# Column quarters for the sums of the front, and the last round, the norm, the gates and the heads' loads in another order

## The chip, the cores and the metric

The kernel runs on one core of a Trainium2 chip. Time is the device time of one execution in microseconds (us); the median over several runs is compared. The core has five engines that each take their instructions in order: PE (matmuls, with weight loads as PEld), VectorE (DVE), ScalarE (ACT), GpSimd (POOL) and SyncE (SP). SP, ACT and POOL also issue DMAs; SP and ACT have hardware queues, POOL a software queue.

## The reference

A trunk of two layers over a sequence of 1024 tokens of width 1024, in float32. Every sub-layer takes `h = rms(x) * g * (1 + scale) + shift`, where scale, shift and gate come from the conditioning vector c by a matrix-vector product (`silu(c) @ w + b`).

```python
# layer 0: S5 mixer
u, z = split(h @ w_in)                      # 1024 -> 2 x 1024
s = scan(abar, bbar @ u); y = C @ s + D * u # 64 groups of 16 channels, 64 complex states
y = gelu(y); y = y * sigmoid(y @ w_glu + b_glu) * silu(z)
x = x + gate * (y @ w_out)
# shared: k, v, forget gates from x;  k = head_rms(k);  F = cumsum(log_sigmoid(f + bias))
# layer 1: attention, 16 heads of 64
q, z = split(h @ w_in); q = head_rms(q) / 8
o = softmax(q k' + F_q - F_k, causal) v;  x = x + gate * ((o * silu(z)) @ w_out)
```

## The kernel before

All activations lie transposed: a strip is 128 channels by 1024 tokens, in two halves of 512 tokens. To keep accuracy with the fast matmul type, every weight and activation is split into a high part (ScalarE's copy, `aH`, `w_hi`) and a low part (VectorE's subtraction, `aL`, `w_lo`), and each product is three matmuls, high by high, high by low, low by high (`project_part`, L108). `weight_strip` (L82) loads a strip of weights through SP and splits it.

The order on each engine is made by the framework's planner: it walks the program with a timeline of estimated costs and gives each engine a fixed order. `tc.issue_after(ins)` adds an edge in that order, on the engine of `ins` alone: what is written inside the block comes behind `ins` on that engine. It is no wait on a semaphore.

The stages, in order of time, with the names in the profile:

1. The front (L127 to L377). For each of eight strips of x, SP loads one matrix of scale weights (`mwx`) and the strip (`xt`); VectorE reduces the product of the matrix with silu(c), a copy of c on all partitions (`gemv`, L131), to 128 values of scale; ScalarE and VectorE make `aH` and `aL` scaled by them, without the norm; ScalarE squares the strip (`sqx`) and PE sums the squares over all channels by a matmul with a constant matrix (`msx`, L298), for both halves. The factor of the norm, `q2x`, is -2/rms, multiplied onto the result of the projections (`et`, L333). The shift is handled as two more token columns (`aH`, `aL`, L311 and L312) next to the second half: PE runs a projection in three chunks of 512, 256 and 258 columns, and the last gives the bias `bi`. Strips 0 to 3 of u are projected before the S5 loop (`U_FIRST`), strips 0 and 1 straight from the front in PSUM tiles of their own (`u01`). Beside it VectorE makes the coefficients of the S5 layer, `dt`, `mag` (a power on POOL, L228), angles `th`, their sine and cosine, powers `pwr`, `pwi`, and the matrices `bb`, `bbs`. They start on VectorE as soon as `ldt`, `are`, `aim` are loaded, and those from `th` on are gated behind `last_lo`, the last shift column.
2. The S5 loop (L680 to L703): eight turns; `products`, `tables`, `scan` and `rotate_back` on VectorE (`moa`, `wm`, `sT`, `r`), small matmuls on PE (`pin`, `pk`, `vps`, `py`), swaps of partition halves by DMA (`v`). `unit()` puts the remaining projections between them, a third of a strip at a time. `taps` (L579) holds matmuls that use 32 columns of PE each, at four places.
3. The gated unit (L752 to L775): `pj_g`, `zt` and `yt` loaded back from memory, `sg`, `zs`.
4. The output projection (L786 to L814), 16 tiles in the order `OUT_SEQ`: all of half 0 is done after the twelfth. `x1` is the new residual; its squares are summed on POOL (`acc`), and `ms` gives the mean of a half.
5. Keys, values, queries (L831 to L970): `modulated` makes `aH` and `aL` of all eight strips and both halves; before it VectorE and POOL in turn multiply `x1` by `q2` in place (L834). Six jobs, `v0 v2 k0 k2 q0 q2`, each of two wide weight strips and eight token tiles (`tkps`, L861, 24 matmuls of 128 x 256). Values go to memory (`vt`, `v_d`), keys and queries are squared, averaged and raised to -1/2 on POOL (`hms`), multiplied (`hnt`), transposed (`trps`), split (`kh`, `kl`) and stored. After `v0` `forget_gates` runs. The other 48 matrices of scale and shift are loaded by `mod_load` and reduced by `mod_take` along stages 3 to 5, 16 of them in `v0` and `v2`. In `q0`, `modulated` runs again for the queries.
6. Attention (L1155 to L1174): 64 steps of one head and 256 queries, two steps of `scores` ahead (`LOOK`). `head` (L989) loads a head's keys, queries and values, mostly by POOL. `some_fill` puts parts of the z projection (`zb`) and of the first rows of the last projection (`f`) between the steps: 8 parts at each of three places at the start, then 2 a step.
7. The last projection (`pj_f`, L1184) and the stores.

The lines that the change touches and what calls them:

Of the kernel before, what the change touches and what calls it, by code (L numbers as in the profile page):

```python
# [37 lines left out]
F_ROWS, Z_END = 2, 2  # L38
# [7 lines left out]
def trunk(tc, a, out):  # L46
# [3 lines left out]
    with top:  # L50
# [20 lines left out]
        vecs = ctile([P, 98], "vecs")  # L71
        c_b = modp.tile([P, D], F32, name="c_b", tag="c_b", bufs=1)
        Q.dma_start(out=c_b, in_=a["c"].broadcast_to([P, D]))
        Q.dma_start(out=vecs, in_=a["vecs"])
        vec, at0 = {}, 0
        for nm, w in (("a_g", 8), ("kv_g", 8), ("b_g", 8), ("b_glu", 8), ("kg", 1), ("qg", 1), ("modb", 64)):
            vec[nm] = vecs[:, at0:at0 + w]
            at0 += w
# [3 lines left out]
        def weight_strip(src, shape, l_eng=None, pool=None):  # L82
            raw = (pool or wpool).tile(shape, F32, name="w_raw", tag="w_raw", bufs=2 if pool else 1)
            Q.dma_start(out=raw, in_=src)
# [5 lines left out]
        def copy_on(eng, o, i):  # L90
            if eng is S:
                S.activation(o, i, AF.Copy)  # L92
# [5 lines left out]
        def split(x, hi, lo, h_eng=None, l_eng=None):  # L98
            copy_on(h_eng or S, hi, x)
            (l_eng or V).tensor_tensor(out=lo, in0=x, in1=hi.bitcast(F32), op=ALU.subtract)  # L100
# [7 lines left out]
        def project_part(ps, w, act, half, ks, k0=0, k1=KT - 1):  # L108
            for k in ks:
                for n, (wt, at) in enumerate(((0, 0), (0, 1), (1, 0))):  # L110
                    T.matmul(ps, w[wt][:, k, :], act[at][k][half], start=(k == k0 and n == 0), stop=(k == k1 and n == 2))  # L111

        def project(w, act, half, nm):
            ps = pj.tile([P, HL], F32, name="pj_" + nm, tag="pj")
            project_part(ps, w, act, half, range(KT))
# [20 lines left out]
        def mod_load(behind):  # L136
            n = mod_next[0]
            if n < 64:
                mw = mwp.tile([P, D], F32, name="modw", tag="modw")
                with tc.issue_after(behind):  # L140
                    Q.dma_start(out=mw, in_=a["modw"][n])
# [30 lines left out]
        def modulated(x, k, i, s, sh, act, pool=None, l_eng=None):  # L172
# [19 lines left out]
        with l0:  # L192
# [8 lines left out]
            S.dma_start(out=ldt, in_=a["log_dt"])  # L201
# [1037 lines left out]
```

## Time and profile before

| | us |
|---|---|
| median of 3 runs | 1207.44 (1205.32 to 1210.37) |
| the profiled execution | 1206.17 |
| its span in the profile | 1204.4 |
| PE busy | 1153.0 (96%), 7414 matmuls |
| VectorE busy | 854.5 (71%) |
| ScalarE busy | 606.3 (50%) |
| POOL busy | 376.0 (31%) |
| granted clock of PE, mean | 0.987 |

A row of instructions begins with its start and duration in us, or, in a grouped view, with its line; then come engine, line, operation and `out<-in`; `xN` is the count; in brackets or behind the bar stand the idle time before it and what released it. A row of stretches gives the length, then for each engine its busy time and (x) its instructions, the granted share of PE's clock, the busy share of the DMA engines and GB/s. Matmuls overlap in the pipeline, so a matmul's duration is longer than the distance to the next one.

### The profile page before, as it was taken

The numbers are of one execution on the slowest core, as the hardware profiler recorded it, in microseconds if no ns is written. First come the engines' busy times: TensorE is split into PE (matmuls) and PEld (weight loads), VectorE is DVE, ScalarE is ACT, GpSimd is POOL, SyncE is SP. The second block draws the span as 40 slices with busy tenths as digits, with TensorE's granted clock in tenths as the row PEclk, the third lists the DMA queues.
The fourth block names the chain that finished last, engine by engine and source line by source line (L and its number), as shares of the span: only waits on it lengthen the run. The fifth ranks groups of instructions, "written<-read, shape, count | busy, mean of one in ns | idle before, by whom it ended". The sixth has DMA issues, their size and how long they took to land.

```text
span 1204.4 us, 20401 instructions
## 1 busy us (share of the span) xinstructions
PE 1153.0 (96%) x7414; PEld 1020.9 (85%) x7414; DVE 854.5 (71%) x1725; ACT 606.3 (50%) x1140; POOL 376.0 (31%) x586
## 2 busy tenths in 40 slices
PE   8989998997999998899999999999999999999898
PEld 6879887886788786889999989998888898888686
DVE  7889899885399877875444664347888788887421
ACT  6666766665335234322223443237677777885310
POOL 4000000000000234510044483437576665764100
PEclk9999999998999999999999999999999999999999
DMA  9754556584976894467524275527696978951342
GB/s 359 222 175 128 164 167 163 158 218 151 328 231 192 281 324 140 148 190 248 179 74 173 106 143 165 131 84 151 102 157 112 136 118 112 155 92 27 100 162 79
DMA packets 110388, 197.09 MB, mean 164 GB/s; under 512 B 17136, under 2 KB 58224, under 8 KB 108752
## 3 DMA queue, kind: packets, MB, share of 16 engines
q1 hardware_dynamic: 83072, 153.25, 40.3%
q0 software_dynamic: 25216, 37.76, 19.4%
q10 hardware_dynamic: 2000, 4.79, 1.6%
q8 instruction: 59, 0.97, 0.4%
q14 instruction: 41, 0.34, 0.1%
HBM read 138.21 MB, written 46.27 MB: 153 GB/s over the span
## 4 chain that ended last, share of the span: by engine, by line
PE 67%; DVE 13%; ACT 8%; DMA 4%; issue 4%; POOL 2%; SPq 1%; ACTq 0%; POOLq 0%; DVEq 0%
PE tkps L861 17%; PE u L274 7%; PE pj_o L111 6%; PE pj_f L111 6%; PE zb L111 5%; PE pj_g L111 5%; PE tp L1065 4%; PE ov L1072 3%; PE ov L1071 3%; PE sp L1033 2%; PE sp L1034 2%; PE z L274 2%; DVE r L207 1%; DVE w_lo L100 1%; PE f L111 1%
## 5 line engine op out<-in xcount | busy, mean ns | idle before, releaser
L861 PE MATMUL tkps<-wvh,aH 128*128 128x256 f32 (+1 forms) x768 | 220.6, 288 | 5.5 <-DVE flog L875 4.8
L861 PE MATMUL tkps<-wvl,aH 128*128 128x256 f32 (+1 forms) x768 | 217.3, 284 | 0.0
L861 PE MATMUL tkps<-wvh,aL 128*128 128x256 f32 (+1 forms) x768 | 217.0, 283 | 0.2 <-POOL aL L177 0.2
L861 PEld LDWEIGHTS tkps<-wvh,aH 128*128 128x128 f32 x768 | 145.9, 190 | 6.9 <-issue 5.4
L861 PEld LDWEIGHTS tkps<-wvl,aH 128*128 128x128 f32 x768 | 146.0, 190 | 0.3 <-issue 0.2
L861 PEld LDWEIGHTS tkps<-wvh,aL 128*128 128x128 f32 x768 | 145.5, 190 | 0.7 <-POOL aL L177 0.4
L1067 ACT ACTIVATE pth<-tp 128x512 fp32r<-128x512 f32 (+1 forms) x192 | 87.0, 488 | 56.8 <-PE ov L1071 30.6
L1040 ACT ACTIVATE pr<-pr,mx 128x128 f32<-128x128 f32 (+7 forms) x128 | 98.8, 773 | 22.6 <-DVE mx L1037 21.1
L1042 POOL TENSOR_SCALAR pr<-pr,sm 128x128 f32<-128x128 f32 (+7 forms) x128 | 95.9, 758 | 43.5 <-DVE sm L1041 41.5
L1068 DVE TENSOR_TENSOR ptl<-tp,pth 128x512 fp32r<-128x512 f32 (+1 forms) x192 | 101.2, 552 | 10.6 <-ACT pth L1067 10.1
L92 ACT ACTIVATE w_hi<-w_raw 128x1024 fp32r<-128x1024 f32 x49 | 51.6, 1054 | 90.5 <-PE pj_f L111 29.1
L1037 DVE CUSTOM_DVE_ANT_0 pr<-sp,msk 128x512 f32<-128x512 f32 (+3 forms) x128 | 72.7, 569 | 23.8 <-PE tp L1065 21.0
L1071 PE MATMUL ov<-pth,vhl 128*128 128x256 f32 x320 | 85.8, 300 | 0.2
L1065 PE MATMUL tp<-ident,pr 128*128 128x128 f32 x576 | 84.2, 275 | 1.1 <-DVE ptl L1068 1.0
L885 ACT ACTIVATE hsq<-tkps 128x256 f32<-128x256 f32 x64 | 24.5, 383 | 116.2 <-PE tkps L861 111.0
L1072 PE MATMUL ov<-ptl,vhl 128*128 128x256 f32 x320 | 81.0, 286 | 0.2
L1065 PEld LDWEIGHTS tp<-ident,pr 128*128 128x128 f32 x576 | 69.3, 141 | 11.5 <-DVE ptl L1068 2.7
L1033 PE MATMUL sp<-kk,qs 128*128 128x256 f32 (+2 forms) x192 | 71.5, 375 | 2.8 <-DVE mx L1037 2.4
L888 POOL TENSOR_TENSOR hms<-hms,nhalf 128x4 f32<-128x4 f32 x64 | 68.7, 1074 | 5.0
L890 DVE TENSOR_TENSOR hnt<-tkps,hms 128x256 f32<-128x256 f32 x64 | 27.0, 422 | 60.2 <-POOL hms L888 60.1
L1034 PE MATMUL sp<-kk,q 66*128 66x256 f32 (+2 forms) x192 | 66.2, 348 | 0.0
L887 POOL TENSOR_SCALAR hms<-hms 128x4 f32<-128x4 f32 x64 | 13.0, 203 | 165.2 <-DVE hms L886 164.1
(328 smaller groups left out, 3264.0 us busy)
## 6 DMA issues: line engine op xcount, KB each, us to landing
modw<-modw SPq DMA_DIRECT2D x48, 512.0 KB
wvr<-kvq_w SPq DMA_DIRECT2D x12, 1024.0 KB
mwx<-modw SPq DMA_DIRECT2D x16, 512.0 KB
w_raw<-a_w_in SPq DMA_DIRECT2D x16, 512.0 KB
v_d<-vt SPq DMA_DIRECT2D x32, 256.0 KB
kk<-k_d POOLq DMA_DIRECT2D x16, 512.0 KB, 7.6
vhl<-v_d POOLq DMA_DIRECT2D x16, 512.0 KB, 8.6
qs<-q_d POOLq DMA_DIRECT2D x32, 256.0 KB, 5.1
```

What stands on the lines that cost most here:

```text
L111: T.matmul(ps, w[wt][:, k, :], act[at][k][half], start=(k == k0 and n == 0), stop=(k == k1 and n == 2))
L274: m = T.matmul(ps[:, 0:c1 - c0], w[wt][:, k, :], act[at][k][i][:, c0:c1], start=(k == 0 and n == 0), stop=(k == KT - 1 and n == 2)).ins
L861: T.matmul(ps[:, 0:nv], at, wt[:, k, 0:nv], start=(n == 0), stop=(n == 3 * KT - 1))
L1033: T.matmul(sp[:, 0:wm_], qsl, kk[:, 0, lo:lo + wm_], start=True, stop=False)
L1034: T.matmul(sp[:, 0:wm_], q1_[:, P * i:P * i + P], kk[0:HD + 2, 1, lo:lo + wm_], start=False, stop=True)
L1040: S.activation(pr[:, 0:nk], pr[:, 0:nk], AF.Exp, scale=-1.0, bias=mx, accum_out=sm)
L1042: G.tensor_scalar(out=pr[:, 0:nk], in0=pr[:, 0:nk], scalar1=sm, scalar2=0.0, op0=ALU.mult, op1=ALU.add)
L1065: T.transpose(out=tp[:, b, :], in_=prs[qi][:, P * (b0 + b):P * (b0 + b) + P], identity=ident)
L1067: S.activation(pth[:, 0:m, dst], tp[:, 0:m, :], AF.Copy)
L1068: V.tensor_tensor(out=ptl[:, 0:m, dst], in0=tp[:, 0:m, :], in1=pth[:, 0:m, dst].bitcast(F32), op=ALU.subtract)
L1071: T.matmul(ov, vhl[:, b, :], pth[:, b - b0, :], start=(b == 0), stop=False)
L1072: end = T.matmul(ov, vhl[:, b, :], ptl[:, b - b0, :], start=False, stop=(b == nb - 1)).ins
```

## The change

In order of the stages:

- Front. The sums of squares of four strips are made together: `quarters` issues four matmuls, each with 32 columns of the constant matrix and a strip of its own, whose outputs lie in four groups of 32 partitions of one PSUM tile; two rounds cover eight strips. A copy to SBUF (`mq`) and one matmul with 1/32 (`o32`) for each half bring the groups together. The eight matrices of the shift are stored in another layout (`mod_sh`) and multiplied on PE by silu(c) in the same way (`psh`, two rounds for each half), copied (`shr`) and brought to columns by eight small matmuls (`pm`), in place of eight of VectorE's reductions. The second weight strip has a raw buffer of its own, and both strips are loaded near the start. The loads and the first small instructions of the coefficients come behind `lo_end`, the last `aL` of the front, and the gate of `th` becomes `lo_end` too; these loads go by POOL, `vecs` by ScalarE. Strips 2 and 3 use the PSUM tiles that strips 0 and 1 leave. B and C are loaded behind the weights of strip 3.
- `neg2_rsqrt` reads PSUM directly and has one ScalarE instruction fewer.
- S5 loop: one more `unit` before the last `states_out`.
- Gated unit and output projection take PSUM tiles from `psa` (three buffers) instead of `pj` (two); loads of z and y are chained in order of use; the mean of half 0 is placed in the middle of the next projection.
- `modulated` multiplies by scale and `q2` in one instruction, adds the shift on ScalarE for the high part and in a second fused instruction for the low one; the products in place and POOL's part fall away. Half 0 for the keys and values runs behind the last `w_lo` of the output projection, half 1 behind value tiles 2 to 5 of `v0`.
- Matrices 16 to 39 are reduced in stages 3 and 4, and 40 to 63 in `v2`, `k0` and `k2`. `v0` has none.
- Values are stored by POOL from four buffers; `forget_gates` runs in steps between tiles of `v2`.
- Heads are loaded by SP, all of them. Eight parts of the z projection come before the last normalisation of `q2`.
- The last projection's row 2 is begun among the fill (`F_ROWS` 3), with its weights in a buffer of the keys, and the last four steps take four parts each (`Z_END` 4).

```diff
-F_ROWS, Z_END = 2, 2
+F_ROWS, Z_END = 3, 4
...
+        def project(w, act, half, nm, pool=None, tag="pj", between=None):
+            ps = (pool or pj).tile([P, HL], F32, name="pj_" + nm, tag=tag)
+            m = project_part(ps, w, act, half, range(KT // 2))
+            if between:
+                with tc.issue_after(m):
+                    m = between()
...
         def neg2_rsqrt(v, r, ps, o):
-            S.activation(v, ps, AF.Identity, bias=eps_t)
-            S.activation(r, v, AF.Ln)
+            S.activation(r, ps, AF.Ln, bias=eps_t)
             S.activation(r, r, AF.Exp, scale=-0.5)
-            V.tensor_tensor(out=v, in0=v, in1=r, op=ALU.mult)
+            V.scalar_tensor_tensor(out=v, in0=ps, scalar=EPS, in1=r, op0=ALU.add, op1=ALU.mult)
...
-            S.activation(act[0][k][i], x[k][:, sl], AF.Identity, scale=s[:, k:k + 1], bias=sh[:, k:k + 1])
-            V.tensor_scalar(out=h, in0=x[k][:, sl], scalar1=s[:, k:k + 1], scalar2=sh[:, k:k + 1], op0=ALU.mult, op1=ALU.add)
-            (l_eng or V).tensor_tensor(out=act[1][k][i], in0=h, in1=act[0][k][i].bitcast(F32), op=ALU.subtract)
+            V.scalar_tensor_tensor(out=h, in0=x[k][:, sl], scalar=s[:, k:k + 1], in1=q2[:, sl], op0=ALU.mult, op1=ALU.mult)
+            S.activation(act[0][k][i], h, AF.Identity, bias=sh[:, k:k + 1])
+            V.scalar_tensor_tensor(out=act[1][k][i], in0=h, scalar=sh[:, k:k + 1], in1=act[0][k][i].bitcast(F32),
+                                   op0=ALU.add, op1=ALU.subtract)
...
+            def quarters(ps, ws, xs, first, last):
+                m = T.matmul(ps[96:P, :], ws[3], xs[3], start=first, stop=last).ins
+                with tc.issue_after(m):
+                    for q in range(3):
+                        T.matmul(ps[32 * q:32 * q + 32, :], ws[q], xs[q], start=first, stop=last)
...
-                for i in range(2):
-                    T.matmul(mps[i], onesm, sq[:, HL * i:HL * i + HL], start=(k == 0), stop=(k == KT - 1))
+                if k % 4 == 3:
+                    for i in range(2):
+                        quarters(mps[i], [onesm[:, 0:32]] * 4, [t[:, HL * i:HL * i + HL] for t in sqs[-4:]], k == 3, k == KT - 1)
...
+            for i in range(2):
+                T.matmul(mps[i], o32, mq[:, HL * i:HL * i + HL], start=True, stop=True)
...
-                last_mod = mod_tile(k)
+                    last_mod = Q.dma_start(out=mws[k], in_=a["mod_sh"][k])
...
+                        quarters(psh, [cs[:, k] for k in range(4 * r, 4 * r + 4)],
+                                 [t[:, HL * c:HL * c + HL] for t in mws[4 * r:4 * r + 4]], r == 0, r == 1)
+                S.activation(shr[:, HL * c:HL * c + HL], psh, AF.Copy)
+            for k in range(KT):
+                T.matmul(pm[:, 2 * k:2 * k + 2], shr[:, P * k:P * k + P], o32[:, 0:2], start=True, stop=True)
...
-            gate.enter_context(tc.issue_after(last_lo))
+            gate.enter_context(tc.issue_after(lo_end))
...
-                    unit(1 if more else 2)
+                    unit(1 if more else 3)
...
-                ps = project(held[e][1], act, i, f"o{e}_{i}")
+                ps = project(held[e][1], act, i, f"o{e}_{i}", psa, "psa", pending)
...
-            for i in range(2):
-                sl = slice(HL * i, HL * i + HL)
-                for k in range(KT):
-                    (G if k % 2 else V).tensor_tensor(out=x1[k][:, sl], in0=x1[k][:, sl], in1=q2[:, sl], op=ALU.mult)
-                    modulated(x1, k, i, s_kv, sh_kv, act, xnp, G if k % 3 == 1 else V)
+            for k in range(KT):
+                with tc.issue_after(last_part):
+                    modulated(x1, k, 0, s_kv, sh_kv, act, xnp)
...
-                vt = wv.tile([P, 4, 2, HD], F32R, name="vt", tag="vt")
+                vt = hp.tile([P, 4, 2, HD], F32R, name="vt", tag="kh" if t % 2 else "kl")
...
+                                if job == "v0" and i == 0 and 2 <= n < 6:
+                                    for k in (2 * n - 4, 2 * n - 3):
+                                        with tc.issue_after(end):
+                                            modulated(x1, k, 1, s_kv, sh_kv, act, xnp)
...
-                            if t % 2:
+                            if t % 2 and job != "v0":
                                 mod_take(end, 1)
-                                mod_load(wide_dma[-1])
+                                mod_load(wide_dma[-1], 8 * KT)
...
+                            if job == "q2" and i and d:
+                                for _ in range(Z_FIRST):
+                                    with tc.issue_after(last_nt[-3]):
+                                        behind_z = next(z_fill)
...
-            G.dma_start(out=kk[0:HD], in_=k_d[:, rows, :].rearrange("a d t -> d a t"))
-            G.dma_start(out=kk[HD:P, 0], in_=k_d[0, rows, :])
+            Q.dma_start(out=kk[0:HD].bitcast(F32), in_=k_d[:, rows, :].rearrange("a d t -> d a t"))
+            Q.dma_start(out=kk[HD:P, 0].bitcast(F32), in_=k_d[0, rows, :])
...
+            if e == 2 and e not in wf:
+                w = at0.tile([P, 2, KT, P], F32R, name="wf2", tag="kk")
+                raw = wpool.tile([P, KT, P], F32, name="w_raw", tag="w_raw", bufs=1)
+                Q.dma_start(out=raw, in_=a["b_w_out"][e])
+                wf[e] = w[:, 0], w[:, 1]
+                split(raw, *wf[e])
```

More of the change, by code (lines that the diff above doesn't have):

```diff
@@ L200, in trunk @@
             ldt = tmp.tile([NG, 1], F32, name="ldt")
-            S.dma_start(out=ldt, in_=a["log_dt"])
-            for hh in range(2):
-                S.dma_start(out=are[64 * hh:64 * hh + 64], in_=a["A_re"])
-                S.dma_start(out=aim[64 * hh:64 * hh + 64], in_=a["A_im"])
             def tt(o, x, y, op, eng=V):
@@ L344, in u_strip @@
                     else:
-                        ps, m = (done[c], None) if c < 2 and done else chunk(w, c, f"u{e}")
+                        ps, m = (done[c], None) if c < 2 and done else chunk(w, c, f"u{e}", tags[c])
                         if c == 2:
```

267 lines of the change are left out of this document (166 added, 101 removed).

## The prediction

> **What bounds the kernel now.** I read the page first, then the busy time by stretches, then who waited for whom, then the timeline around each hole.
>
> ```profile
> span 1204.4 us, 20401 instructions
> ...
> PE 1153.0 (96%) x7414; PEld 1020.9 (85%) x7414; DVE 854.5 (71%) x1725; ACT 606.3 (50%) x1140; POOL 376.0 (31%) x586
> ```
>
> PE, at 96%, is the bound. The change removes hardly any matmul, so its worth is the time in which PE stands still, and the time in which it runs at half its clock behind such a hole. These stretches show both; the column after POOL is the granted clock.
>
> ```profile
> 60.00:75.00 15.00, 11.83 (x62) 10.04 (x61) 13.92 (x45) 9.97 (x23) 0.00 (x0) 0.89 0.50 160
> 125.00:140.00 15.00, 13.50 (x88) 11.22 (x87) 12.75 (x16) 9.83 (x16) 0.78 (x1) 0.89 0.55 169
> 265.00:290.00 25.00, 18.13 (x111) 16.63 (x110) 11.16 (x12) 8.57 (x13) 1.06 (x2) 0.86 0.57 186
> 320.00:335.00 15.00, 12.73 (x55) 9.99 (x54) 8.37 (x12) 4.26 (x6) 0.00 (x0) 1.00 0.99 303
> 475.00:500.00 25.00, 19.00 (x105) 15.82 (x104) 23.82 (x29) 9.70 (x15) 16.47 (x13) 0.93 0.43 132
> 500.00:545.00 45.00, 41.34 (x323) 40.13 (x322) 32.40 (x59) 15.01 (x27) 11.37 (x7) 0.96 0.62 197
> 650.00:700.00 50.00, 50.00 (x402) 48.74 (x401) 33.33 (x58) 23.53 (x38) 22.89 (x31) 1.00 0.23 87
> 755.00:770.00 15.00, 12.29 (x92) 12.09 (x92) 6.38 (x10) 3.49 (x6) 9.05 (x14) 0.89 0.77 176
> 800.00:825.00 25.00, 23.71 (x144) 20.68 (x142) 16.57 (x53) 12.41 (x31) 11.00 (x22) 0.86 0.30 107
> 1120.00:1136.00 16.00, 12.37 (x61) 8.57 (x61) 8.54 (x13) 5.02 (x9) 2.46 (x4) 1.00 0.33 114
> ```
>
> Behind the length come the busy times of PE, the weight loads, VectorE, ScalarE and POOL. A hole costs the length less PE's busy time, plus the length times the missing share of the clock: at 60: 3.2 + 1.7 = 4.9 us; 125: 1.5 + 1.7 = 3.2; 265: 6.9 + 3.5 = 10.4; 320: 2.3; 475 to 545: 6.0 + 3.7 idle and 1.8 + 1.8 clock = 13.3; 755: 2.7 + 1.7 = 4.4; 800: 1.3 + 3.5 = 4.8; 1120: 3.6. That is 47 us, and a better order of the same work can gain little more. What ended these holes (total, count and longest, in us):
>
> ```profile
> PE py L639 <- DVE r L207: 8.2, 3, 6.9
> PE pk L579 <- DVE moa L207: 5.0, 6, 1.7
> PE tkps L861 <- DVE flog L875: 4.8, 3, 1.8
> PE pj_o L111 <- DVE w_lo L100: 4.1, 2, 3.0
> PE trps L897 <- DVE hnt L890: 3.2, 3, 2.7
> ```
>
> In all five VectorE was late; work for PE was there.
>
> The Trainium skill, "TensorE: Matmul & The Clock Gate", Part 1, has the half clock follow idle gaps of about its window, some 3.4 us. Here it also followed the stretch at 755, with 2.7 us of idle time in all. By that rule the 1.7 us of clock there would not hang on the hole, and the sum below would be 1.7 us smaller; the trace's row decides.
>
> **The front, to the start of the S5 loop.** The first fence is from the chain of waits, the others from the timeline.
>
> ```profile
> 17.58 1.76 PE msx L298 x4
> ```
>
> ```profile
> 85.11 0.60 PE L567 MATMUL pin<-ident,wm 128*128 128x128 f32 x4
> 85.64 0.43 PE L579 MATMUL pk<-moa,bb 128*32 128x128 f32 x8
> 85.99 0.40 PE L581 MATMUL pk<-dd,ident 128*128 128x16 f32 x2
> ...
> 90.30 1.92 PE L604 MATMUL vps<-uu,min__963 128*128 128x128 f32 x15
> ```
>
> ```profile
> 9.58 10.58 POOL L228 TENSOR_TENSOR mag<-ebase,adt 128x64 f32<-128x64 f32 x1 [3.23 <-DVE adt L207]
> ...
> 35.17 1.41 DVE L293 SCALAR_TENSOR_TENSOR aL<-xt,s_a,aH 128x512 fp32r<-128x512 f32 x2 [1.51 <-ACT aH L292]
> ...
> 50.37 0.21 DVE L207 TENSOR_TENSOR th<-aim,dt 128x64 f32<-128x64 f32 x1
> ```
>
> The mean of squares takes 1.76 us per strip of x today, 14.1 us for eight. The kernel already has matmuls on column quarters: four of them (L579, eight records) start at 85.64 and the next full one (L581) at 85.99, so 0.35 us; eight records of that width on the whole array (L604, 0.128 each) would be 1.02. Quarters run beside each other, at 0.34 of the full price. A group of four at 512 columns costs at least 0.88 us (two records at msx's 0.44) and at most 3.52 (all eight in a row); scaled by 0.34 it is 1.2, which I take. Four groups for the mean (4.8), two closing matmuls (1.8), four groups for the shift (4.8) and 16 small records at L604's price (2.1) are 13.5 against 14.1. PE gains 0.6 us; at the bounds it gains 3.2 or, serial, loses 18.
>
> VectorE loses eight of sixteen reductions; the same one elsewhere (L131, quoted below) takes 1.22 us: 9.8 us off. The small coefficient work moves from before the end of L293 (36.6) to behind it, and the coefficient chain, which today starts at 50.4 (th, behind the last shift columns), can start near 38. Queued behind the new wait are the power on POOL, 10.6 us (mag), now from about 38 to 49, and all that needs it. B and C stand one weight load later in SP's queue, ScalarE gives its first load to vecs, and the coefficients' loads move from ScalarE's queue to POOL's; none of these is needed before 49. But pin (85.1) also needs PE to be through strips 0 to 3. From 36.6 on PE's work was 48.5 us with the hole of 4.9. In the new order PE enters with about 3 us more of strips 0 and 1 done, and has the closing matmuls, the shift and 1.2 us groups ahead of it. So I take 1 us of gain, bounds -3 and 4; if VectorE's 9.8 us covered nothing, 0.
>
> **The S5 loop and its end.** With VectorE some 8 us ahead, part of the waits of pk (5.0) and of the hole at 125 (3.2) goes: 5, bounds 0 and 9. At 265 one more third of a strip stands before the last output, so it covers part of py's 6.9 us: 3 of 10.4, bounds 0 and 7.
>
> **Gated unit and output projection.** Three PSUM buffers instead of two, and z's loads chained ahead of y's: the 2.3 us at 320, bounds 0 and 3.
>
> **From the output projection into the values.** Timeline first, then the chain, then the groups by line:
>
> ```profile
> 469.28 1.06 ACT L92 ACTIVATE w_hi<-w_raw 128x1024 fp32r<-128x1024 f32 x1 [3.19 <-PE pj_o L111]
> ...
> 503.79 0.38 ACT L872 ACTIVATE vt<-tkps 128x256 fp32r<-128x256 f32 x1 [6.42 <-DMA v_d<-vt]
> ```
>
> ```profile
> 479.75 1.15 DVE w_lo L100
> 480.89 0.04 issue
> 480.94 6.78 PE pj_o L111 x22
> ```
>
> ```profile
> L131 DVE CUSTOM_DVE_ANT_0 modw<-modw,c_b 128x1024 f32<-128x1024 f32 x48 | 58.4, 1216 | 0.0
> ...
> L834 DVE TENSOR_TENSOR x<-x,q2x 128x512 f32<-128x512 f32 x8 | 10.5, 1371 | 0.0
> ```
>
> VectorE is full (23.8 of 25 us), partly with products beside POOL's (L834, 1371 ns each). So w_lo, whose w_hi was ready at 470.3, comes at 479.75, and PE waits. The change takes away the sixteen products (10.5 us on VectorE, the rest on POOL), some 16 reductions of this stretch (19.5 us), and the store that held vt for 6.42 us, now on POOL's queue with four buffers instead of two. A modulated tile now costs VectorE two fused instructions of 0.71 us (L293). Half 0's eight are ordered behind the last w_lo, near 472; 11.4 us of them and some 3 us of other work end near 486. PE, without its 6.0 us of holes, runs out of output projection near 482, and can follow the tiles one by one. What is late next is the last modulated tiles, by some 3 us: I take 10 of the 13.3, bounds 2 and 13. Half 1 lies beside eight value tiles and costs nothing; without that cover it would cost another 11 us.
>
> The 24 reductions that move into v2, k0 and k2 take 29 us there. VectorE is busy 33 of 50 us in k2 (650 to 700), so they fit, but one can push an hnt back by 1.2 us, and hnt frees PE's buffer. I charge 3 us, bounds 0 and 20.
>
> **Queries and heads.**
>
> ```profile
> 754.61 1.17 POOL L997 DMA_DIRECT2D qs<-q_d  x2 [4.29 <-DMA q_d<-kh]
> ...
> kk<-k_d POOLq DMA_DIRECT2D x16, 512.0 KB, 7.6
> ```
>
> At 755 POOL waits for stores and issues loads before it computes the power that hnt needs; on SP these loads delay no power: 4.4 gained. Eight parts of the z strips ahead of the last normalisation are 24 matmuls, cover for the hole at 800: 3 of 4.8. Bounds for both: 0 and 9. SP now issues seven DMAs a head in order, some behind waits for kk's buffers, and the z strips' weights stand behind them. A step is (1120 - 800) / 64 = 5 us, and a landing (7.6 us) has four steps of cover: no cost there.
>
> **The end.** Row 2's first half (24 matmuls) covers the 3.6 us at 1120, and its weights come earlier: 3, bounds -3 and 3.6.
>
> **Sum.** 1 + 5 + 3 + 2.3 + 10 - 3 + 4.4 + 3 + 3 = 28.7. For small waits that a wholly new order opens I take 4 us off (an estimate, the size of one hole above): 25. The profiled execution took 1206.2 (its span and 1.8 around it); less 25 is 1181. The runs' median, 1207.4, lies 1.3 above it, less than I can resolve; I keep 1181.
>
> **Rivals.**
> 1. *The quarters run one after another.* PE loses 18 instead of gaining 0.6, in the front where it is needed: 1200. For it: L579's are 128 columns wide, these 512. Against it: 0.35 us. Chance 0.05. The Trainium skill, "TensorEngine Tiling", Key Properties, says that a change of tiling mode drains the engine; the row's 0.35 us already holds one change back, so the trace leaves that little room.
> 2. *VectorE is ahead in the loop and that buys nothing*, because PE reaches pin no earlier: 1181 + 1 + 5 = 1187 or, with the hole at 265 unchanged, 1190. Chance 0.15.
> 3. *The moved reductions are paid at the keys*: sixteen more than v2's eight, 1.2 us each, in front of an hnt: 16 us more than charged, 1197. Against it: VectorE has a third of its time free there. Chance 0.12.
> 4. *Slower: SP's one queue paces the attention.* If the loads of a pair of heads stand behind a buffer wait and the weights behind them, each of the seven later pairs pays a whole landing: 1181 + 7 x 7.6 = 1234. It decides against the change from 3.8 us a pair, where the 26 us to 1207 are used up. Against it: the four steps. Chance 0.07.
> 5. *The change does not do what it says*: planned anew, the holes open elsewhere: 1204. Chance 0.06.
>
> The forecast (its own range 1165 to 1190) has 0.55.
>
> **How the numbers follow.** Below 1165 needs nearly all of the 47 us; beyond 1202 lie rivals 4 and 5 and little else: range 1165 to 1202. A measurement of this kernel tells 0.5%, 6 us, from no change. Faster than 1201 are the forecast and rivals 1 to 3 with most mixtures, 0.86; within 6 us 0.07; slower 0.07.
>
> **What would show it.** Right: a group of four quarters near 1.2 us; th before 40; a clock over 0.97 in the stretches that answer to 475, 500, 755 and 800; no POOL DMA ahead of hms; PE idle under 30 us in all. Wrong: pin later than 86; holes before tkps in the k jobs ended by hnt; SP waiting on kk with PE idle in zb; PE idle before the last rows as now.

## The result and the profile after

The changed kernel takes 1188.88 us (median of 4 runs, 1188.02 to 1190.74) against 1208.61 us (1205.32 to 1210.37): ratio 0.984, 95% interval 0.982 to 0.987. Measured again later on another chip, the ratio was 0.985 (0.981 to 0.988). The forecast was 1181. The profiled spans went from 1204.4 to 1186.2, so 18.2 us are to be found, where the steps had promised 28.7, and 25 after the allowance. The page of the changed kernel:

```profile
span 1186.2 us, 20506 instructions
...
PE 1148.3 (97%) x7486; PEld 1017.5 (86%) x7486; DVE 845.9 (71%) x1713; ACT 607.1 (51%) x1141; POOL 318.6 (27%) x524
```

I cut both executions at the first matmul of `pin`, `pj_g`, `pj_o`, `trps`, `sp` and `f`, which gives seven stages: front, S5 loop, gated unit, output projection to values, keys and queries, attention, end. First the kernel before, then the changed one, stretches in order; the columns are those explained under the profile of before.

```profile
0.00:85.10 85.10, 78.07 (x406) 62.54 (x407) 70.46 (x169) 53.72 (x96) 15.32 (x28) 0.98 0.77 260
85.10:295.30 210.20, 194.66 (x1426) 174.81 (x1425) 177.57 (x218) 134.04 (x207) 5.30 (x15) 0.98 0.60 166
295.30:387.20 91.90, 89.63 (x387) 71.95 (x386) 71.25 (x110) 41.65 (x60) 0.00 (x0) 1.00 0.76 239
387.20:602.00 214.80, 203.13 (x1266) 180.47 (x1265) 154.77 (x216) 69.81 (x105) 58.27 (x50) 0.98 0.66 216
602.00:807.20 205.20, 201.97 (x1635) 197.81 (x1634) 102.92 (x190) 66.41 (x117) 98.46 (x143) 0.99 0.43 127
807.20:1073.90 266.70, 262.67 (x1677) 232.33 (x1676) 220.08 (x701) 201.87 (x478) 176.94 (x312) 0.99 0.79 126
1073.90:1204.40 130.50, 122.92 (x629) 101.01 (x627) 57.49 (x127) 38.78 (x80) 21.75 (x40) 1.00 0.31 92
```

```profile
0.00:88.10 88.10, 81.90 (x478) 65.19 (x479) 63.27 (x153) 55.58 (x98) 18.37 (x34) 0.94 0.74 255
88.10:291.80 203.70, 193.12 (x1426) 173.15 (x1425) 176.83 (x217) 134.87 (x208) 5.14 (x15) 0.99 0.62 170
291.80:381.10 89.30, 89.30 (x387) 72.11 (x386) 73.85 (x113) 43.31 (x62) 0.00 (x0) 1.00 0.78 254
381.10:583.90 202.80, 198.49 (x1265) 177.84 (x1264) 129.13 (x175) 67.54 (x101) 54.67 (x69) 1.00 0.56 189
583.90:790.40 206.50, 200.97 (x1636) 196.73 (x1635) 124.43 (x232) 65.23 (x117) 84.12 (x126) 1.00 0.50 161
790.40:1056.40 266.00, 262.11 (x1678) 231.51 (x1677) 220.21 (x700) 202.13 (x478) 136.62 (x243) 0.99 0.57 126
1056.40:1186.20 129.80, 122.38 (x629) 101.00 (x627) 58.15 (x127) 38.50 (x80) 19.70 (x39) 1.00 0.28 93
```

The lengths alone tell where the time went; the forecast's steps stand beside them:

| stage | gain, us | by the steps |
|---|---|---|
| front | -3.0 | 1 |
| S5 loop and its end | 6.5 | 5 + 3 |
| gated unit | 2.6 | 2.3 |
| output projection to values | 12.0 | 10 |
| keys and queries | -1.3 | 4.4 - 3 |
| attention | 0.7 | 3 |
| end | 0.7 | 3 |
| sum | 18.2 | 28.7 |

Each side of this table is a single execution. In the runs below that leave the loop as the change has it, the loop took 203.7 to 208.8 us with nearly the same idle time of PE (10.6 to 12.3 us), so its gain of 6.5 could as well have been 1.4: most of the difference is half clock. With the new front `pin` comes at 86.8 to 88.2. The other stages agree within some 3 us from run to run where no edit touches them.

PE stands idle 51.4 us before (span less busy time) and 37.9 after: 13.5 us. The other 4.7 us are busy time, from 1153.0 to 1148.3 with nearly the same matmuls: the mean granted clock rose from 0.987 to 0.991. So about a quarter of the gain is clock, in these two executions.

The places of the old holes, in the changed kernel:

```profile
270.00:295.00 25.00, 23.29 (x152) 21.05 (x151) 16.86 (x22) 15.21 (x24) 1.07 (x2) 1.00 0.63 210
...
455.00:490.00 35.00, 30.69 (x160) 24.69 (x159) 30.68 (x36) 15.82 (x24) 13.42 (x13) 1.00 0.24 78
490.00:535.00 45.00, 45.00 (x377) 44.92 (x376) 21.10 (x37) 15.33 (x26) 8.39 (x16) 1.00 0.50 176
637.00:665.00 28.00, 22.47 (x166) 20.71 (x165) 24.86 (x48) 9.27 (x17) 9.96 (x12) 1.00 0.29 95
735.00:755.00 20.00, 20.00 (x173) 20.00 (x172) 10.28 (x19) 6.82 (x12) 8.36 (x14) 1.00 0.77 234
785.00:805.00 20.00, 18.95 (x110) 16.38 (x110) 13.29 (x44) 9.33 (x24) 8.24 (x18) 0.83 0.37 132
```

The holes of 500 and 755 are filled, that of 265 is down to 1.7 us and that of 475 to 4.3 us, the half clock of the first heads is still there (0.83), and there is a new hole of 5.5 us at 637 to 665. What PE waited for (total, count, longest):

```profile
PE pk L641 <- DVE moa L213: 5.0, 6, 1.7
PE tkps L931 <- DVE hnt L960: 3.1, 1, 3.1
PE py L701 <- DVE r L213: 3.1, 3, 1.7
PE tkps L931 <- ACT aH L185: 2.8, 2, 1.5
...
PE zb L113 <- DVE aL L186: 2.4, 1, 2.4
```

### The profile page after: what moved, and what is told of

It is laid out like the page before. It is cut to its first block, busy times and chain, and to the rows that moved or that the text cites. A ratio compares the mean times of both kernels' runs of the same rounds, so it can differ in the third digit from the quotient of the medians.

```text
span 1186.2 us, 20506 instructions
## 1 busy us (share of the span) xinstructions
PE 1148.3 (97%) x7486; PEld 1017.5 (86%) x7486; DVE 845.9 (71%) x1713; ACT 607.1 (51%) x1141; POOL 318.6 (27%) x524
## 4 chain that ended last, share of the span: by engine, by line
PE 77%; DVE 11%; ACT 7%; issue 3%; DMA 2%; SPq 0%; ACTq 0%; DVEq 0%
PE tkps L931 22%; PE pj_g L113 8%; PE u L261 7%; PE pj_o L113 6%; PE zb L113 6%; PE pj_f L113 5%; PE tp L1157 4%; PE ov L1163 2%; PE ov L1164 2%; PE z L261 2%; PE sp L1125 2%; PE f L113 2%; PE sp L1126 2%; ACT pr L1132 2%; DVE ptl L1160 1%
## 5 line engine op out<-in xcount | busy, mean ns | idle before, releaser
L1157 PEld LDWEIGHTS tp<-ident,pr 128*128 128x128 f32 x576 | 69.4, 142 | 13.5 <-DVE ptl L1160 4.6
L1163 PEld LDWEIGHTS ov<-pth,vhl 128*128 128x128 f32 x320 | 60.5, 189 | 3.2 <-DVE oc L1170 2.0
L1164 PEld LDWEIGHTS ov<-ptl,vhl 128*128 128x128 f32 x320 | 60.7, 190 | 3.0 <-DVE ptl L1160 2.8
```

What stands on the lines that cost most here:

```text
L1157: T.transpose(out=tp[:, b, :], in_=prs[qi][:, P * (b0 + b):P * (b0 + b) + P], identity=ident)
L1163: T.matmul(ov, vhl[:, b, :], pth[:, b - b0, :], start=(b == 0), stop=False)
L1164: end = T.matmul(ov, vhl[:, b, :], ptl[:, b - b0, :], start=False, stop=(b == nb - 1)).ins
```

## The experiments

All start from the changed kernel and are planned anew by the framework. Ratios are against the kernel before, on the same chip; the changed kernel's is 0.984 to 0.985, so 0.001 is 1.2 us. The theory at the start was that each stage's gain or loss has a cause of its own, as in the table.

**The front undone.** The whole front as before: full-array sums, shift by VectorE, old order of the coefficients.

```diff
-                        quarters(mps[i], [onesm[:, 0:32]] * 4, [t[:, HL * i:HL * i + HL] for t in sqs[-4:]], k == 3, k == KT - 1)
+                    T.matmul(mps[i], onesm, sq[:, HL * i:HL * i + HL], start=(k == 0), stop=(k == KT - 1))
...
-            gate.enter_context(tc.issue_after(lo_end))
+            gate.enter_context(tc.issue_after(last_lo))
...
```

> The changed kernel with the front of before (sums and shift as they were, coefficients in their old order), all else changed. Theory: the S5 loop runs in step with its first matmul, pin, so the change's front, whose pin came at 88.1 us instead of 85.1, costs 3 us: pin is near 85 again, every scan 3.3 us earlier than in the changed kernel, the hole of py stays small (under 3 us), and the time is 1186. Rival: the new front's earlier VectorE work is what made the hole at the loop's end small; then py waits some 7 us again and the time is 1190 to 1193.

Measured: 1196.32 us (1193.91 to 1197.46), ratio 0.992 (0.990 to 0.994), some 9 us above the changed kernel. My theory fell, and the time is above the rival's too. `pin` came at 88.6 us, not near 85, so this run does not tell what the new front costs: its first strips were loaded later than in the kernel before (the second square starts at 15.1 us against 12.9; why, stays open), two stretches ran at half clock from 15.6, and `pin` itself waited 2.9 us for `wm` of VectorE. From `pin` to `pj_g` it took 213.1 us against 203.7, more than the spread between runs; `py` waited 4.8 us at the loop's end. The last swap of the loop shows a part of that; the product that follows it, in the kernel before, the changed one and this run (in brackets what VectorE waited for it):

```profile
276.43 1.23 DVE L207 TENSOR_TENSOR sT<-sT,v 128x1024 f32<-128x1024 f32 x1 [5.46 <-DMA v<-v]
```

```profile
277.54 1.23 DVE L213 TENSOR_TENSOR sT<-sT,v 128x1024 f32<-128x1024 f32 x1 [3.27 <-DMA v<-v]
```

```profile
285.82 1.22 DVE L217 TENSOR_TENSOR sT<-sT,v 128x1024 f32<-128x1024 f32 x1 [6.21 <-DMA v<-v]
```

So with the new front the last swap is 2 to 3 us less late. In SP's queue a load of 512 KB of weights goes ahead of it, by 2.6 us in the kernel before and 4.0 us in the changed one, in this order:

```profile
267.11 0.66 SPq L84 DMA_DIRECT2D w_raw<-a_w_glu  x1
269.73 1.14 SPq L521 DMA_DIRECT2D v<-v  x2
```

```profile
269.07 0.66 SPq L86 DMA_DIRECT2D w_raw<-a_w_glu  x1
273.04 1.16 SPq L583 DMA_DIRECT2D v<-v  x2
```

The other runs fit. Behind the load by 2.5 us (this run), VectorE's wait is 6.2 us; by 3.1 and 3.2 (the two runs with 33 matmuls below), 5.0 and 4.7; by 3.9 or more (all others), 3.3 to 3.8. Two unrelated edits moved the spacing and the wait went with it. No run moves the spacing alone, so the runs support that the load delays the swap, but do not show it by itself.

**The sums on the whole array, alone.** Only the mean of squares goes back; the shift stays on quarters.

```diff
-                if k % 4 == 3:
-                    for i in range(2):
-                        quarters(mps[i], [onesm[:, 0:32]] * 4, [t[:, HL * i:HL * i + HL] for t in sqs[-4:]], k == 3, k == KT - 1)
+                for i in range(2):
+                    T.matmul(mps[i], onesm, sq[:, HL * i:HL * i + HL], start=(k == 0), stop=(k == KT - 1))
```

> The changed kernel with the sums of squares on the whole array again, strip by strip (sixteen matmuls of 128 columns, 14.1 us), instead of quarters and two closing matmuls (3.5 + 1.8 us); the shift stays on quarters. Theory: PE works without a break from 11.4 to 39 us in the changed kernel, so the 8.8 us of matmuls more come on top: strip 2 begins 5 to 9 us later, pin is at 93 to 97, and the time is 5 to 9 us above the changed kernel's. Rival: the loads set the pace of the strips and the matmuls fit between them, as they did before the change: pin within 1.5 us of 88, the same time.

Measured: 1192.53 us (1190.63 to 1195.45) beside 1189.89 for the changed kernel in the same set; `pin` at 89.4. Of 8.8 us of matmuls, 1.3 arrive at `pin`: the rival as to the front. The median is 2.6 us above, but the five times of each overlap, so "the same time" is neither shown nor refuted; 5 to 9 us is unlikely. While the strips come in, the DMA engines are full (share 1.03 between 11 and 38 us in both runs), and in this run no stretch was at half clock, while the changed kernel's mean clock there is 0.87. So part of the quarters' gain was paid back in clock: in the two profiles of the new front with a whole clock there (the runs with two thirds, and with spread products and four thirds, below) `pin` came at 86.8 and 86.9, 2.5 us before this run's.

**The start without half clock.** 33 matmuls on constants ahead of the first strip instead of 28.

```diff
-            for _ in range(28):
+            for _ in range(33):
```

> The changed kernel with 33 instead of 28 matmuls on constants at the start, so that PE is busy until the first strip is there (11.4 us). Theory: the two stretches of half clock from 12.5 to 19.3 us followed PE's idle time from 9.8 to 11.4; without it the clock is whole there, PE is through strips 0 and 1 some 1 to 3 us earlier, pin comes at 85.5 to 87, and the time is 1 to 3 us below the changed kernel's. Rival: the front is paced by the loads of the strips, so that pin stays at 88 whatever the clock does, and the time is the same.

Measured: 1189.97 us (1187.34 to 1191.73), ratio 0.987 (0.984 to 0.989). The clock was whole from 11.4 to 22.1 us, `pin` came 0.9 earlier, and nothing arrived at the end: `py` waited 3.2 us at the loop's end instead of 1.7. The rival again. That the 33 matmuls kept the clock whole is not shown: the two profiles just named had a whole clock there with 28, and an earlier `pin`. PE begins on the first strip anywhere between 10.7 and 11.4 us, and the clock behind it differs from run to run.

**One third of a strip less at the loop's end.**

```diff
-                    unit(1 if more else 3)
+                    unit(1 if more else 2)
```

> The changed kernel with two thirds of a strip instead of three before the last output of the S5 loop. Theory: the third (12 matmuls of 0.23 us, 2.8 us) covers the wait for the last swap: without it py waits 4 to 5 us instead of 1.9, the clock halves behind it for one or two stretches of 3.4 us, and the time is 1192 to 1195. Rival: the hole became small because the last swap by DMA came back 2 us sooner, and the third only moved work: 1189.

Measured: 1194.63 us (1192.79 to 1197.17), ratio 0.991 (0.989 to 0.993). The wait of `py` is 4.9 us, and the clock falls with it (270 to 295: PE busy 20.11 us, clock 0.86). The theory holds: one third is worth some 5 us of the profiled span (1191.6 against 1186.2): 3.2 of idle time, and clock. The other 2.0 us of the 6.9 in the kernel before are gone here too: VectorE waits 3.5 us for the last swap, as in the changed kernel, against 5.5.

**The reductions in their old places.**

```diff
-        def mod_load(behind, end=5 * KT):
+        def mod_load(behind, end=8 * KT):
...
-                            if t % 2 and job != "v0":
+                            if t % 2:
```

> The changed kernel with the 48 reductions of scale and shift in their old places (two taken after each tile of the output projection, eight in v0), all else changed. Theory of the prediction: VectorE was full between 475 and 500, and the reductions taken out of there are a large part of the 12 us gained from the output projection to the keys: PE idles some 6 us more there and halves its clock once or twice: 1195 to 1199. Rival: the products that fell away were enough by themselves, 1188 to 1190; and if the reductions in the keys' jobs made the new hole at 642, that hole is gone and the time is 1184.

Measured: 1195.83 us (1194.03 to 1198.05), ratio 0.992 (0.990 to 0.994). From `pj_o` to the first `trps` it took 209.0 us against 202.8 in the changed kernel (and 214.8 before): the reductions are 6 of the 12 us gained there; the other parts of the change make the rest, and which of them was not tried. The profiled span is 10.1 us longer, but 5.1 of that lie in the S5 loop, which the edit does not touch (208.8 us, mean clock 0.97), so the theory is read from the stage, not from the time. The hole at 642 stayed with no reduction near it (PE idle 3.7 us from 620 to 690, against 5.5; `trps` waited for `hnt`), so the reductions do not make it.

**The queries' products spread.** In the changed kernel eleven of the sixteen fused products of the queries stand in a row on VectorE, ahead of an `hnt` that PE needs. Two rows of VectorE and two of PE:

```profile
637.90 7.38 DVE L184 SCALAR_TENSOR_TENSOR x<-x,s_b,q2x 128x512 f32<-128x512 f32 x11
645.19 0.42 DVE L960 TENSOR_TENSOR hnt<-tkps,hms 128x256 f32<-128x256 f32 x1
...
645.66 0.39 PE L931 MATMUL tkps<-wvh,aH 128*128 128x256 f32 x1 [3.11 <-DVE hnt L960]
...
651.61 0.50 PE L113 MATMUL zb<-aL,w_hi 128*128 128x512 f32 x1 [2.41 <-DVE aL L186]
```

```diff
-                            with tc.issue_after(k0_end):
+                            with tc.issue_after(last_nt[8 * i + k - 16]):
                                 modulated(x1, k, i, s_b, sh_b, act)
...
-                            if t % 2 and job != "v0":
-                                mod_take(end, 1)
+                            if job == "k0" or t % 2 and job != "v0":
+                                mod_take(end, 0 if job == "k0" and i and d and t == 7 else 1)
```

> The changed kernel with the queries' sixteen products by scale and norm let in one by one, each behind one token tile of k2, and sixteen reductions taken in k0 instead of eight there and eight in k2, so that the scale is ready when k2 begins. Theory: the new hole at 642 to 652 us (3.1 us before tkps by hnt, 2.4 us before zb by aL) comes from eleven such products standing in a row on VectorE ahead of an hnt; spread, PE idles under 1 us between 620 and 690 and the time is 1183 to 1184. Rival: the moved reductions delay hnt; then k0, which now has twice as many, shows holes before tkps, and the time is 1188 or more.

Measured: 1183.61 us (1182.35 to 1188.62), ratio 0.983 (0.980 to 0.985), though k0 now has twice the reductions. The same stretch, changed kernel first:

```profile
620.00:690.00 70.00, 64.47 (x510) 61.94 (x509) 56.38 (x99) 26.78 (x45) 27.29 (x37) 1.00 0.49 167
```

```profile
620.00:690.00 70.00, 68.47 (x538) 65.84 (x537) 53.41 (x94) 28.18 (x47) 33.29 (x42) 1.00 0.39 144
```

5.5 us of idle time became 1.5, a little more than the 1 that I expected. With the run before it, where the block stood and no reductions did, the block of products is the cause. The profiled span fell by 5.6 us; by the ratios it is about 2 us, within their intervals.

**The fill held back on PE.** The first 24 parts of the z projection come behind the last matmul of the queries, on PE.

```diff
-                                    with tc.issue_after(last_nt[-3]):
+                                    with tc.issue_after(last_nt[-3]), tc.issue_after(tk_end[0]):
                                         behind_z = next(z_fill)
...
-                some_fill(Z_FIRST)
+                with tc.issue_after(tk_end[0]):
+                    some_fill(Z_FIRST)
...
```

> The changed kernel with the first 24 parts of the z projection held back on PE behind the last matmul of the queries; in the changed kernel they stand behind an instruction of VectorE, which does not hold a matmul, and PE ran all 72 matmuls between 648 and 705, before the heads. Theory: so placed they do what the edit was meant to do, PE's idle time and half clock at the first heads (4.9 and 3.4 us between 775 and 801) shrink to under 3 together, the wait of zb at 649 (2.6 us) is gone, and the time is 4 to 6 us below the changed kernel's. Rival: between 640 and 705 VectorE is the slower engine and those 72 matmuls (16.7 us) were what PE had to do meanwhile: then tkps waits for hnt several us longer there, and the time is the same or worse.

Measured: 1194.28 us (1191.59 to 1196.86), ratio 0.990 (0.987 to 0.993). My theory was right at the first heads, where PE has no hole and a whole clock; the rival was right in the keys and queries, where PE waits and the clock falls to 0.93 (620 to 690), and on the time. One row of its stretches, one of its waits:

```profile
785.00:820.00 35.00, 35.00 (x196) 29.92 (x195) 19.29 (x67) 19.30 (x45) 13.14 (x22) 1.00 0.40 106
```

```profile
PE trps L969 <- DVE hnt L962: 5.2, 2, 3.0
```

The 72 matmuls were the cover of the queries' products; taken to the heads, they are missed more than they help, by 3.3 us of the two stages together (475.8 against 472.5). The rest of the profiled span's 8.9 us is not the edit's as far as the trace shows: 4.2 lie in the S5 loop, which it does not touch.

**The heads' loads on POOL.**

```diff
-            Q.dma_start(out=kk[0:HD].bitcast(F32), in_=k_d[:, rows, :].rearrange("a d t -> d a t"))
+            G.dma_start(out=kk[0:HD].bitcast(F32), in_=k_d[:, rows, :].rearrange("a d t -> d a t"))
...
-                Q.dma_start(out=qs[HD * r:HD * r + HD].bitcast(F32), in_=q_d[r, rows, :])
+                G.dma_start(out=qs[HD * r:HD * r + HD].bitcast(F32), in_=q_d[r, rows, :])
...
```

> The changed kernel with the heads' keys, queries and values loaded by POOL again, as before the change. Theory of the prediction: POOL's loads of the first heads wait for stores in front of the powers that hnt needs, as at 755 in the kernel before; a hole of some 2.9 us and a stretch of half clock (1.7) come back ahead of the last transposes, 4 to 5 us above the changed kernel. Rival: with the values' stores on POOL and eight parts ordered ahead, the loads no longer meet the powers: the same time.

Measured: 1193.35 us (1190.74 to 1195.11), ratio 0.989 (0.986 to 0.991), 5 us above. POOL again waits for a store of the queries in front of the powers:

```profile
744.01 1.16 POOL L1104 DMA_DIRECT2D qs<-q_d  x2 [2.82 <-DMA q_d<-kh]
745.24 0.19 POOL L957 TENSOR_SCALAR hms<-hms 128x4 f32<-128x4 f32 x1
745.49 1.07 POOL L1104 DMA_DIRECT2D qs<-q_d  x2
746.58 1.03 POOL L958 TENSOR_TENSOR hms<-hms,nhalf 128x4 f32<-128x4 f32 x1
```

`trps` waits 3.4 us for `hnt`. The prediction's step holds.

**The end as before.**

```diff
-F_ROWS, Z_END = 3, 4
+F_ROWS, Z_END = 2, 2
```

> The changed kernel with two rows of the last projection begun among the steps instead of three, and two parts instead of four in the last four steps, as before. Prediction: row 2's half covers the 3.6 us of waits around 1120, so that without it the time is 3 us above. Rival, by the trace of the changed kernel: that cover was bought with a wait of ov for ptl (1.8 us at 1070) and of tp (1.0 at 1106), and the stretch from the first f to the end became only 0.9 us shorter: 0 to 1 us above.

Measured: 1189.15 us (1188.04 to 1190.14), ratio 0.986 (0.983 to 0.988): 1 us or nothing, as the rival said, but not for its reason. From the first `f` to the end it is 129.6 us against 129.8; `f` waits 1.6 us for `oc` and `aH`, of the 3.6 that PE stood idle around 1120 before; with three rows PE idles 1.6 us there as well, for other tiles. The 1.7 us of `ov` behind `ptl` are there with two rows as with three. So the third row did not bring that wait; which other part did stays open.

**Two versions that go further.** The spread products, with four thirds before the loop's last output; then the same with 33 matmuls at the start; and the changed kernel beside them.

```diff
-                    unit(1 if more else 3)
+                    unit(1 if more else 4)
```

> The changed kernel with the queries' products spread over the tiles of k2 (as in the run that did this alone) and four thirds of a strip before the last output of the S5 loop instead of three. Theory: the fourth third (2.8 us) covers what is left of py's wait (1.9 to 2.5 us), and the gated unit's first matmuls, which need the last strip of y only 5 us after they begin, do not notice: 2 us below the spread kernel alone, about 4 to 5 below the changed kernel. Rival: the thirds behind the loop were needed to cover the way of the last y through memory; then PE waits before pj_g instead, and the time is that of the spread kernel.

> The same as the run before it (products spread, four thirds) with 33 matmuls on constants at the start instead of 28. Theory: without the half clock at 12.5 to 19.3 pin comes 0.9 us earlier, as in the run that did this alone, and the loop's end, now covered by the fourth third, does not take it back: 1 us below that run. Rival: as there, the last swap lands later by what was won, and the time is the same.

> The changed kernel itself, on the same chip as the three runs before it, so that they can be compared with it directly: 1186 to 1190 us by its first measurement.

Measured in this order: 1182.36 us (1182.2 to 1185.25), ratio 0.980 (0.977 to 0.983); 1183.86 (1182.32 to 1184.88), 0.981 (0.977 to 0.984); 1189.89 (1184.35 to 1192.61), 0.985 (0.981 to 0.988). With four thirds the loop's end has no hole left, and `pj_g` begins at 290.1 without one:

```profile
270.00:295.00 25.00, 25.00 (x161) 22.48 (x160) 17.75 (x22) 14.69 (x25) 1.06 (x2) 1.00 0.62 208
```

The first of them beats both kernels, the changed one by 7.5 us. What the fourth third adds to the spread products alone is not shown: the two profiled spans are equal (1180.6 us), the intervals of the ratios overlap. The 33 matmuls add nothing, as their rival said.

## Why the prediction was right or wrong

The side and the kind were right: the matmuls stayed, the gain was idle time and clock, and 1188.9 lies in the range. The forecast was 7.9 us too low: four terms were too large (front, loop, heads, end) and a hole was new, some 17 us together; two terms that were too small (the loop's end, the output projection) gave 6 of it back, and the allowance 4. That errors of both signs offset each other, so that the time lies in the range, is in part luck.

- *Front, 1 us: wrong, -3.0.* The group of four was sized well. In the changed kernel's timeline the two groups of a round (two halves, so four records for each strip) run from 22.12 to the next matmul at 23.97, 0.93 us a group; I took 1.2, with 0.88 as the lower bound.

```profile
22.12 0.62 PE L278 MATMUL msx<-sqx,onesm 128*32 128x512 f32 x1
22.12 0.63 PE L281 MATMUL msx<-sqx,onesm 128*32 128x512 f32 x3
...
23.97 0.97 PE L261 MATMUL u<-aH,w_hi 128*128 128x512 f32 x4
```

  The step that failed is "PE enters with about 3 us more of strips 0 and 1 done": it entered strip 2 only 1.9 us earlier, because the loads paced the strips and two stretches ran at half clock. Behind that point the shift's groups and small matmuls, 5.7 us, stand on PE with no wait to hide in, where VectorE's reductions had cost PE only the hole of `bi`. `th` came at 40.17, a little late by my sign, and `pin` at 88.11, which by my own sign ("later than 86") says wrong. In no run with the new front was it earlier than 86.8.
- *Loop, 5 us: wrong, none.* `pk` waited 5.0 us before and 5.0 after, the hole of 125 stands as it was (PE idle 1.7 us from 128 to 143, clock 0.89), and every scan came 3.3 us later (103.60 and 106.85 the first, 267.41 and 270.72 the last). That VectorE was ahead bought nothing there, which is rival 2. Its place was right; that its numbers, 1187 and 1190, are also the closest is luck, since they keep my terms for the heads and the end. That the loop's end would gain more than I charged was in neither.
- *The loop's end, 3 of 10.4: too small, 7.0.* Idle time went from 6.9 to 1.7 us and the clock from 0.86 to 1.00. But the hole was not worth 10.4: my sum counts the half clock also while PE stood idle (0.00 us busy from 274 to 278, at a clock of 0.73), and only half of its 3.5 us fell on matmuls, so that it cost 8.7. The other holes of the sum hardly have this fault. The third of a strip is some 5 of the gain (the run with two thirds); the other part, the earlier landing of the last swap, was in no step.
- *Gated unit, 2.3: right, 2.6.* PE has no idle time there any more; whether by the third buffer or by the order of the loads was not tried.
- *Output projection to values, 10: right, 12.0.* Late next were indeed the last modulated tiles (`tkps` behind `aH`, 2.8 us; 4.3 us idle between 455 and 490). The price of a tile was wrong: I took 0.71 us for each fused instruction, but the first took 1.6 us here, beside POOL's work, as the rows in the last section show.
- *Reductions -3, queries 4.4: together 1.4, measured -1.3.* The hole at 755 is gone, and POOL's loads bring it back. The reductions cost at most 1 us: without any in this stage (their old places) it took 205.5 us against 206.5, and with twice as many in k0 (the spread run) the time fell, so rival 3 is out. What failed is a term that I did not have: `modulated` for the queries, two fused instructions of 0.75 us for each of sixteen tiles, planned in a block. My sign, holes before `tkps` ended by `hnt`, pointed at the right place for another reason.
- *Heads, 3 of 4.8: wrong, 0.7.* "Eight parts of the z strips ahead of the last normalisation are cover": they stand behind an instruction of VectorE, and such an edge orders one engine, as the description of the kernel says. PE ran them 100 us earlier. Where they did reach the heads, the cover was missing elsewhere. And most of the 4.8 was clock, which was not a matter of cover alone: in the spread run the same stretch, uncovered, had a whole clock, and attention took 264.5 us instead of 266.0.
- *End, 3: wrong, 0.7.* The cover for "the 3.6 us at 1120" had little left to cover: without the third row `f` waits 1.6 us, with it PE idles 1.6 us there all the same, and a new wait of `ov` for `ptl` (1.7 us) stands among the steps either way.
- *The allowance of 4 us for new small waits* was of the right kind and too small: the new hole of 5.5 us alone is more.

No sign of rival 1 or 4: quarters run beside each other, and in attention PE is idle 3.9 us of 266, with SP issuing all loads. Rival 5 came true in part, with the one new hole. PE's idle time of 37.9 us is above the 30 that I had asked for, and the clock of 0.83 at the first heads is below the 0.97.

## What to carry to other kernels

Ask of each instruction freed on a helper engine whether PE reaches the same point earlier: the loop ran in step with PE, and being ahead there was worth nothing, while one third of a strip put in front of a late transfer was worth 5 us. When a part is rewritten for one place, price it at its other call too: the fused `modulated` won at the values and opened a hole of 5.5 us at the queries, until it was spread over the tiles. Check on which engine an ordering edge acts before counting the work behind it as cover.

## What the runs showed of the hardware

**A hole's price depends on where it falls.** The granted clock changes in steps of 3.41 us. The wait of `pk` near 207 us is the same in two runs (1.74 us). With 33 matmuls at the start, cut at those steps:

```profile
202.88:206.29 3.41, 3.26 (x26) 2.86 (x25) 3.41 (x6) 2.51 (x3) 0.00 (x0) 1.00 0.53 121
206.29:209.70 3.41, 1.67 (x20) 1.45 (x20) 3.41 (x6) 2.26 (x6) 0.00 (x0) 1.00 0.83 262
209.70:213.11 3.41, 3.41 (x14) 3.02 (x14) 3.31 (x4) 1.86 (x4) 0.00 (x0) 0.50 0.29 45
```

And in the changed kernel:

```profile
203.66:207.08 3.42, 3.02 (x24) 2.61 (x23) 3.42 (x6) 2.71 (x4) 0.00 (x0) 1.00 0.59 144
207.08:210.49 3.41, 1.91 (x21) 1.71 (x22) 3.41 (x6) 2.31 (x6) 0.00 (x0) 1.00 0.83 240
210.49:213.90 3.41, 3.41 (x20) 2.87 (x19) 3.31 (x4) 1.50 (x4) 0.00 (x0) 1.00 0.45 89
```

Where PE was busy 1.67 us of a step, the next step ran at half clock (14 matmuls, not 20); where the same hole was cut in two, 1.91 us of a step, it did not. The Trainium skill, "TensorE: Matmul & The Clock Gate", Part 1, says that the window is free-running, 3413 ns long, and that the clock falls after an idle window. The steps agree with the first; for the second, half a window of idle time was enough here. At the first heads of the changed kernel the clock fell behind a step in which PE was busy 2.36 of 3.41 us (790.70 to 794.11), more than the 1.91 above. So busy time as the profile has it is not all that counts. In the spread run, with as much idle time at the same heads (PE busy 18.52 of 20 us, 780.2 to 800.2; 18.95 in the changed kernel, 785 to 805), the clock stayed whole. It also shows in the times: the five runs of the changed kernel in the last set go from 1184.35 us (mean clock 0.994) to 1192.61 (0.989), so part of the spread between runs, and of any single profile's account, is probably the place of the steps.

**VectorE is slower beside POOL.** The fused product of `modulated` in the changed kernel, between 462 and 485 us, where POOL runs tensor operations, and between 637 and 655, where POOL works only on tiles of 128 x 4:

```profile
L184 DVE SCALAR_TENSOR_TENSOR hmod<-x,s_kv,q2x 128x512 f32<-128x512 f32 x8 | 12.5, 1598 | 0.0
```

```profile
L184 DVE SCALAR_TENSOR_TENSOR x<-x,s_b,q2x 128x512 f32<-128x512 f32 x16 | 10.9, 745 | 0.0
```

The same work takes twice as long in the first (1598 ns against 745). The kernel before had it too, in its products of 1371 ns beside POOL's. The other eight products of the first line, from 489 us on, while POOL only issues stores, took 742 to 752 ns. Beside the slow eight POOL ran four tensor operations, 7.3 us while they lasted together; the eight took 6.8 us longer than at 745 ns. No run takes POOL's work away, so that it is the cause is argued from these places.
